# Weight pool first in SBUF, tiles begun at multiples of 2048 bytes, and a 2 KB scratch for dynamic DMAs

## The chip, the cores and the metric

The kernel runs on one core of one Trainium2 chip. The metric is the device time of one execution in microseconds (us); lower is better. Before the change the median of 3 runs was 2548.22 us (2548.09 to 2548.79).

## The reference

Two transformer blocks, one after the other, on 256 tokens of width 2048, all in float32. Cut to what matters here:

```python
# block 1
h = rms_norm(x, norm_mix_w);  proj = h @ w_in            # 2048 x 6160
y_a = chunked_band_attention(...);  y_g = rms_norm(gated_linear_attention(...)) * silu(r_g)
x = x + concat([y_a, y_g]) @ w_out                       # 2048 x 2048
u = causal_depthwise_conv(rms_norm(x) @ w_ffn_up)        # 2048 x 11264
x = x + (gelu(u_gate) * u_val) @ w_ffn_down              # 5632 x 2048
x = x + sigmoid(rms_norm(x) @ w_ple_gate) * (p @ w_ple_proj)
x = rms_norm(x, final_norm_w)
# block 2
z = rms_norm(x) @ w_in_2                                 # 2048 x 7168
x = x + concat([moba_attention(...), silu(rg) * retention(...)]) @ w_o_2
x = x + (silu(h2 @ w_gate_2) * (h2 @ w_up_2)) @ w_down_2
x = x + (p_2 @ w_ple_proj_2) * sigmoid(rms_norm(x) @ w_ple_gate_2 + b_ple_gate_2)
```

Nearly all the work is in the products with weight matrices, every one of which is read once.

## The kernel before

**Numbers in two parts.** Each float32 operand of a large product is split into a high part (rounded to the type fp32r, which TensorE multiplies in one pass) and a low part (the rest, also fp32r). A product is high times high, plus low times high, plus high times low.

**The weight stream.** The weights lie in HBM in the order of use, as 881 tiles of 128 partitions x 1024 numbers (4096 bytes in a partition). `load` (L148) brings one into a buffer `raw` (4 buffers), `split_hi` (L156, ScalarE) makes the high part `wh` (5 buffers), `split_lo` (L167, VectorE) the low part `wl` (4 buffers). Each call of `slot` does this for tiles some places ahead, so that TensorE finds its tile ready. The order of all instructions on all engines is written by the program itself, in one pass.

**The activations.** The other operand of each product lies in a *region*, a tile of 128 partitions x 8 x 2 x 256 numbers (16 KB in a partition): 8 k-tiles, each of 2048 bytes, the high part of 256 tokens and then the low part. There are five places for regions, R0 to R4, used again and again under other names:

| place | names that stand in it, in order of use (the profile leaves the numbers at a name's end out: f10, f11, f22, f23 are all f; g102 is g; hp0 is hp) |
|---|---|
| R0, R1 | h0a, h0b; f10, f11; hp0, hp1; R1: keys and queries; y2a, y2b; g200, g201 and g210, g211 |
| R2 | y1a; g102, g112; m2a; f22; hp2 |
| R3 | keys and queries; g103, g113; m2b; f23; hp3 |
| R4 | the gated linear attention's tiles; y1b; g104, g114; keys and queries; g204, g214 |

**The two forms of product.** All of them go through `mm` (L222), and each matmul loads its own stationary operand (LDWEIGHTS).

- *Narrow* products, `prod_b` (names `acc<-f,wh`, `acc<-f,wl` and so on): the weights are stationary, 128 x 128 (512 bytes in a partition), the activations move. For each k-tile and each of 2 blocks of output columns there is a pair: a matmul of 512 columns (stationary from `wh`, moving the whole k-tile) and one of 256 columns (stationary from `wl`, moving its high half).
- *Wide* products, `prod_a` (names `acc<-wh,m2a` and so on): the activations are stationary, 512 or fewer columns of a weight tile move. For each k-tile and half of the tokens there are three matmuls: `wh`, `wl`, `wh`.

`prod_p`, in the per-layer embedding, is narrow with 256 columns: for each stationary tile the moving operand is first the high half, then the low half of a k-tile of `ph`, then the high half again.

**Where a tile lies.** A pool hands out space in the order in which its tags are first asked for, each at a multiple of 32 bytes. The pools open in the order `sp` (all tiles but the weights'), `wp` (`raw`, `wh`, `wl`), above a scratch of 16,384 bytes for dynamic DMAs and 128 bytes of constants. Adding up the sizes gives each tile's first byte in its partition: R0 begins at 16,384 + 128 + 1,984 (vec) + 512 (ident) + 512 (ones) + 16,384 (X) = 35,904. A k-tile is 2048 bytes, a stationary slice 512, a weight tile 4096, so that all k-tiles of a region, and all slices of a tile, have the same remainder by 128.

Of the kernel before, what the change touches and what calls it, by code (L numbers as in the profile page):

```python
# [5 lines left out]
F32 = mybir.dt.float32  # L6
# [6 lines left out]
P = 128  # L13
# [6 lines left out]
NEG = -1e30  # L20
MIX_ORDER = (0, 1, 2, 3, 8, 9, 10, 11, 4, 5, 6, 7, 12, 13, 14, 15)
HALVES = ((0, 24), (24, 44))


def weight_plan():
    """The weight tiles in the order of use: (k-tiles, column ranges).

    Wide tiles have 2 k-tiles of 512 columns (moving operand), narrow ones
    4 k-tiles of 256 columns (stationary operand).
    """  # L30
    tiles = []
    full = tuple(range(KT))

    def gemm(n, kts, chunks):
        for ch in chunks:
            for i in range(0, len(kts), n):
                tiles.append((kts[i : i + n], ch))

    def even(name, lo, hi, step):
        return [[(name, c, c + step)] for c in range(lo, hi, step)]  # L40

    def wide(name, lo, hi):
        gemm(2, full, even(name, lo, hi, 512))

    def narrow(name, lo, hi, kts=full):
        gemm(4, kts, even(name, lo, hi, 256))

    def ffn(gate, up, off, down):
        for a, b in HALVES:
            gemm(4, full, [[(gate, c * P, c * P + P), (up, off + c * P, off + c * P + P)] for c in range(a, b)])  # L50
            narrow(down, 0, D, tuple(range(a, b)))

    def ple(gate, proj):
        for c in range(0, D, 512):
            narrow(gate, c, c + 512)
            gemm(2, (0, 1), even(proj, c, c + 512, 512))

    gemm(2, full, [[("w_in", 4096, 4608)], [("w_in", 4608, 4864)], [("w_in", 4864, 5120), ("w_in", 6144, 6160)]])
    narrow("w_in", 3072, 4096)
    narrow("w_in", 0, 2048)  # L60
    wide("w_in", 2048, 3072)
    wide("w_in", 5120, 6144)
    narrow("w_out", 0, D, MIX_ORDER)
    ffn("w_ffn_up", "w_ffn_up", FF, "w_ffn_down")
    ple("w_ple_gate", "w_ple_proj")
    wide("w_in_2", 0, 3072)
    narrow("w_in_2", 3072, 5120)
    wide("w_in_2", 5120, 7168)
    narrow("w_o_2", 0, D)
    ffn("w_gate_2", "w_up_2", 0, "w_down_2")  # L70
    ple("w_ple_gate_2", "w_ple_proj_2")
    return tiles


def plan_offsets(tiles):
    out, off = [], 0
    for kts, ch in tiles:
        f = len(kts) * sum(b - a for _, a, b in ch)
        out.append((off, f))
        off += P * f  # L80
    return out, off
# [16 lines left out]
class Net:  # L98
# [4 lines left out]
    def __init__(self, nc, tc, pools, ins, out):  # L103
        self.nc, self.tc = nc, tc
        self.sp, self.wp, self.ps = pools
        self.ins, self.out = ins, out
        self.plan = weight_plan()
        self.offs, _ = plan_offsets(self.plan)
        self.i = 0
        self.raw, self.H, self.L = {}, {}, {}  # L110
        self.ev, self.side = [], []
        self.done = set()
        self.nacc = 0
        self.forced = []

# [1 line left out]
    def t(self, tag, shape, dt=F32, bufs=1, name=None):  # L117
        return self.sp.tile(shape, dt, tag=tag, name=name or tag, bufs=bufs)

    def psum(self, tag, bufs):  # L120
        return self.ps.tile([P, 512], F32, tag=tag, name=tag, bufs=bufs)
# [10 lines left out]
    def pv(self):  # L132
        return self.psum("pv", 1)

# [1 line left out]
    def cut(self, i, part):  # L136
        f = self.offs[i][1]
        return slice(0, f) if part is None else slice(part * f // 2, (part + 1) * f // 2)
# [37 lines left out]
        assert len(self.plan[i][0]) == nk  # L176
        return self.H.pop(i), self.L.pop(i), self.offs[i][1] // nk

# [1 line left out]
    def step(self, q, g):  # L180
        try:
            next(g)
        except StopIteration:
            q.remove(g)
# [25 lines left out]
        while key not in self.done:  # L210
            yield

# [1 line left out]
    def begin_chunk(self):  # L214
        c = self.nacc
        self.nacc += 1
        if c >= 2:
            self.need(("acc", c - 2))
        return c, self.acc()
# [45 lines left out]
                    self.mm(o, x[:, ls], H[:, sl], False, g + j == nk - 1)  # L265

    def join(self, acc, dst):
        """dst = the sum of both halves of a narrow chunk's accumulators."""
        m = self.v2(self.t("tq", [P, 512], bufs=2))
        self.nc.scalar.activation(m, acc[:, :, T:], AF.Copy)  # L270
        yield
        self.nc.vector.tensor_add(dst, m, acc[:, :, :T])
# [4 lines left out]

        self.ev.append(self.freeing(c, evict(acc)))

# [1 line left out]
    def v2(self, ap):  # L281
        return ap.rearrange("p (b t) -> p b t", b=2)

# [43 lines left out]
    def acts_of(self, regions, n, key):  # L327
        return [(regions[k // 8][:, k % 8].rearrange("p a t -> p (a t)"), (key, k)) for k in range(n)]
# [34 lines left out]

        return rc, rb, run()

# [1 line left out]
    def consts(self):  # L367
        nc, ins = self.nc, self.ins
        self.vec = self.t("vec", [P, NV])
        self.ident = self.t("ident", [P, P])  # L370
        self.ones = self.t("ones", [P, P])
        nc.gpsimd.memset(self.ones, 1.0)
        nc.scalar.activation(self.ident[:, 0:1], self.ones[:, 0:1], AF.Copy)
        nc.scalar.dma_start(self.vec[:, 0:16], ins["vec"][:, 0:16])
        self.X = self.t("X", [P, KT, T])
# [69 lines left out]
        while self.ev or self.side:  # L445
            self.tick()

# [1 line left out]
    def mix1(self, acts):  # L449
        nc = self.nc  # L450
        rc, rb = self.rc, self.rb
# [335 lines left out]
        self.done.add(("go", 3))  # L787
        yield

# [1 line left out]
    def ffn(self, blk):  # L791
        nc = self.nc
        hk = self.hkey
        acts = self.acts_of(self.hR, KT, hk)
        regs = (2, 3, 4) if blk == 1 else (0, 1, 4)
        hn = (0, 1) if blk == 1 else (2, 3)
        rb, rskey = self.rb, (hk, "rs")
        key = f"p{blk}"
        for half, (a, b) in enumerate(HALVES):
            G = [self.region(r, f"g{blk}{half}{r}") for r in regs]  # L800
            gk = f"g{blk}{half}"
            for c in range(a, b):
                ev = self.ev_glu1 if blk == 1 else self.ev_glu2
                self.chunk("B", acts, ev(c, c - a, G, gk, rb, rskey))
            gacts = self.acts_of(G, b - a, gk)
            if half:
                self.side.append(self.embed(blk))
                if blk == 1:
                    self.side.append(self.rope_tables())
                R = [self.region(r, f"hp{r}") for r in hn]  # L810
                sq = self.new_sq()
                self.rc, self.rb, rs = self.row_scale(sq, (key, "rs"))
            for c in range(8):
                n, acc = self.begin_chunk()
                self.prod_b(gacts, acc)
                if half:
                    self.ev.append(self.ev_resid(n, acc, c, R, sq, "norm_ple_w" if blk == 1 else "g_ple_2", key, rs))
                else:
                    self.ev.append(self.ev_add(n, acc, c))
        self.hR, self.hkey = R, key  # L820
# [52 lines left out]
            yield from self.put_g(G, gk, cl, w[:, 1, :])  # L873
        return ev

# [1 line left out]
    def embed(self, blk):  # L877
        nc = self.nc
        s8 = self.t("S8a", [P, 2, 1024], name="pr")
        ph = self.t("S8b", [P, 4, 2, T], F32R, name="ph")  # L880
        pr = self.v2(s8[:, 0, 0:512])
        nc.sync.dma_start(pr, self.ins[f"pT{blk}"])
        self.emb = s8, ph
        for _ in range(12):
            yield
        nc.scalar.activation(ph[:, 0:2, 0, :], pr, AF.Copy)
        yield
        nc.vector.tensor_sub(ph[:, 0:2, 1, :], pr, ph[:, 0:2, 0, :].bitcast(F32))
        self.done.add(("emb", blk))
# [82 lines left out]
            yield  # L972
        self.done.add(("ple", blk, c))

# [1 line left out]
    def rope_tables(self):  # L976
        nc, ins = self.nc, self.ins
        tabs = self.tabs = self.t("g4", [P, 4, 2, P], name="tabs")
# [332 lines left out]
def pack(inputs):  # L1311
    g = {k: np.asarray(v) for k, v in inputs.items()}
    mats = {k: g[k][0] for k in (
        "w_in", "w_out", "w_ffn_up", "w_ffn_down", "w_ple_gate", "w_ple_proj", "w_in_2", "w_o_2",
        "w_gate_2", "w_up_2", "w_down_2", "w_ple_gate_2", "w_ple_proj_2")}
    plan = weight_plan()
    offs, total = plan_offsets(plan)
    flat = np.empty(total, np.float32)
# [28 lines left out]


def body(nc, tc, ins, out):
    with tc.tile_pool(name="sp", bufs=1) as sp, tc.tile_pool(name="wp", bufs=1) as wp, \  # L1350
            tc.tile_pool(name="ps", bufs=1, space=PSUM) as ps:
        with tc.manual_schedule():
            net = Net(nc, tc, (sp, wp, ps), ins, out)
            net.build()
    return net
# [16 lines left out]
```

## Time and profile before

| | before |
|---|---|
| median of 3 runs | 2548.22 us (2548.09 to 2548.79) |
| span of the profiled execution, first to last instruction | 2547.2 us |
| the profiled execution's time as the runs count it | not given on the page; the runs' median is 1.0 us above its span |
| TensorE (PE) busy | 2534.5 us, 100% of the span |
| weight loads of TensorE (PEld) busy | 2184.4 us, 86% |
| VectorE (DVE) busy | 1668.3 us, 65% |
| ScalarE (ACT) busy | 1282.9 us, 50% |
| GpSimd (POOL) busy | 8.3 us |
| weight DMAs, share of the 16 engines' time | 54.1% |
| granted TensorE clock, mean | 0.999 |

TensorE's matmuls are pipelined, so that the lengths of neighbours overlap and "busy" says only that no gap was left. What a matmul costs is read from the distance between starts: so many matmuls between two starts, so much time.

### The profile page before, as it was taken

How to read it: one execution, taken by the hardware profiler on the slowest of the kernel's cores; microseconds unless marked ns; L12 is line 12 of the kernel's file. 1: busy time of each engine (PE TensorE's matmuls, PEld its weight loads, DVE VectorE, ACT ScalarE, POOL GpSimd, SP SyncE). 2: the span in 40 equal slices, each digit the busy share in tenths (PEclk: the TensorE clock that was granted, in tenths of full speed). 3: DMA queues.
4: the chain of work that ended last, by engine and by line, in shares of the span. 5: the costliest groups of instructions: out<-in, count | busy, mean ns of one | idle time of the engine just before them, and what ended most of it. 6: DMA issues, size and time to landing. Idle time of an engine off the chain costs nothing.

```text
span 2547.2 us, 36496 instructions
## 1 busy us (share of the span) xinstructions
PE 2534.5 (100%) x14162; PEld 2184.4 (86%) x14162; DVE 1668.3 (65%) x2374; ACT 1282.9 (50%) x1713; POOL 8.3 (0%) x60
## 2 busy tenths in 40 slices
PE   8999999999999999999999999999999999999999
PEld 7887788888888888888878888888888888888888
DVE  6655567777755777767886775666666555666665
ACT  6534544655543565545544544444444334444443
POOL 0000000000000000000000000000000000000000
PEclk9999999999999999999999999999999999999999
DMA  7545355555555555555555455555555555555554
GB/s 242 183 142 178 131 177 188 187 186 190 190 189 188 186 190 190 192 193 187 189 174 188 161 177 189 174 187 189 188 188 189 190 190 189 187 188 193 190 193 147
DMA packets 133550, 469.30 MB, mean 184 GB/s; under 512 B 14960, under 2 KB 17392, under 8 KB 133376
## 3 DMA queue, kind: packets, MB, share of 16 engines
q1 hardware_dynamic: 133232, 466.95, 54.1%
q8 instruction: 111, 1.82, 0.3%
q14 instruction: 63, 0.52, 0.1%
q10 hardware_dynamic: 144, 0.01, 0.0%
HBM read 464.80 MB, written 2.10 MB: 183 GB/s over the span
## 4 chain that ended last, share of the span: by engine, by line
PE 99%; DMA 0%; DVE 0%; ACT 0%; issue 0%; SPq 0%; ACTq 0%
PE acc L222 95%; PE sc L222 2%; PE pv L222 1%; PE tr L650 0%; DMA raw<-weights 0%; PE sc L1099 0%; ACT wh L156 0%; PE sc L1182 0%; PE sc L528 0%; DVE ty L948 0%; SPq L390 0%; DVE wl L167 0%; DVE X L949 0%; PE tr L737 0%; SPq L148 0%
## 5 line engine op out<-in xcount | busy, mean ns | idle before, releaser
L167 DVE TENSOR_TENSOR wl<-raw,wh 128x1024 fp32r<-128x1024 f32 (+1 forms) x881 | 1068.8, 1214 | 830.6 <-PE acc L222 538.6
L156 ACT ACTIVATE wh<-raw 128x1024 fp32r<-128x1024 f32 (+1 forms) x881 | 924.7, 1050 | 905.7 <-PE acc L222 729.8
L222 PE MATMUL acc<-f,wh 128*128 128x512 f32 x2816 | 984.3, 393 | 0.0
L222 PE MATMUL acc<-f,wl 128*128 128x256 f32 x2816 | 786.2, 279 | 0.0
L222 PEld LDWEIGHTS acc<-f,wh 128*128 128x128 f32 x2816 | 528.0, 187 | 123.9
L222 PEld LDWEIGHTS acc<-f,wl 128*128 128x128 f32 x2816 | 528.3, 188 | 0.0
L222 PE MATMUL acc<-g,wh 128*128 128x512 f32 x1408 | 491.0, 393 | 0.0
L222 PE MATMUL acc<-g,wl 128*128 128x256 f32 x1408 | 393.2, 279 | 0.0
L222 PEld LDWEIGHTS acc<-g,wh 128*128 128x128 f32 x1408 | 264.1, 188 | 61.1
L222 PEld LDWEIGHTS acc<-g,wl 128*128 128x128 f32 x1408 | 264.3, 188 | 0.0
L222 PE MATMUL acc<-hp,wh 128*128 128x512 f32 x512 | 179.9, 394 | 0.0
L222 PE MATMUL acc<-hp,wl 128*128 128x256 f32 x512 | 143.0, 279 | 0.0
L222 PEld LDWEIGHTS acc<-hp,wh 128*128 128x128 f32 x512 | 96.0, 188 | 22.2
L222 PE MATMUL acc<-wh,m2b 128*128 128x512 f32 x320 | 104.5, 398 | 0.0
L222 PE MATMUL acc<-wh,m2a 128*128 128x512 f32 x320 | 104.4, 399 | 0.0
L222 PEld LDWEIGHTS acc<-hp,wl 128*128 128x128 f32 x512 | 96.1, 188 | 0.0
L849 ACT ACTIVATE ty<-tU,vec 128x256 f32<-128x256 f32 x88 | 48.1, 595 | 75.1 <-DVE tU L845 75.1
L270 ACT ACTIVATE tq<-acc 128x512 f32<-128x512 f32 x124 | 71.9, 580 | 4.9 <-PE acc L222 4.9
L222 PE MATMUL acc<-wh,h0a 128*128 128x512 f32 (+2 forms) x224 | 68.1, 380 | 5.7 <-ACT wh L156 5.7
L222 PEld LDWEIGHTS acc<-wh,m2a 128*128 128x128 f32 x320 | 60.3, 188 | 14.2
L222 PEld LDWEIGHTS acc<-wh,m2b 128*128 128x128 f32 x320 | 60.1, 188 | 14.1
L222 PE MATMUL acc<-h0a,wh 128*128 128x512 f32 x192 | 68.6, 397 | 0.0
(272 smaller groups left out, 2780.6 us busy)
## 6 DMA issues: line engine op xcount, KB each, us to landing
raw<-weights SPq DMA_DIRECT2D x863, 512.0 KB, 3.4
raw<-weights SPq DMA_DIRECT2D x10, 256.0 KB, 2.8
raw<-weights SPq DMA_DIRECT2D x8, 272.0 KB, 2.8
aB<-bias SPq DMA_DIRECT2D x8, 256.0 KB, 3.5
X<-xT SPq DMA_DIRECT2D x7, 256.0 KB, 6.6
dk<-decay SPq DMA_DIRECT2D x8, 192.0 KB, 3.7
out<-X SPq DMA_DIRECT2D x6, 256.0 KB, 2.8
pr<-pT SPq DMA_DIRECT2D x2, 256.0 KB, 4.2
```

The lines of the kernel that those rows point to most:

```text
L156: self.nc.scalar.activation(self.H[i][:, a], self.raw[i][:, a], AF.Copy)
L167: self.nc.vector.tensor_sub(self.L[i][:, a], r[:, a], self.H[i][:, a].bitcast(F32))
L222: self.nc.tensor.matmul(out, lhsT, rhs, start=start, stop=stop, skip_group_check=True, **kw)
L270: self.nc.scalar.activation(m, acc[:, :, T:], AF.Copy)
L849: nc.scalar.activation(y[:, b, :], u[:, b, 0:T], AF.Identity, scale=self.col("cw0", j), bias=self.col("b_ffn_conv", j))
```

## The change

The pool of the weights is opened first. Scratch for dynamic DMAs shrinks from 16,384 to 2,048 bytes. `t` keeps count of the space handed out, and puts a filling tile ahead of each new tile of 8192 bytes or more, so that it begins at a multiple of 2048; the same is done once ahead of the weight pool. No instruction is added, removed or moved: the streams of all engines read the same but for line numbers and the numbers at the ends of names. What differs is the addresses. (The diff also drops a docstring and some comments; those pieces are left out below.)

```diff
+ALIGN = 2048
+SCRATCH = 2048
...
         self.forced = []
-
-    # ---- tiles ----
+        self.sizes = {}
+        self.off = SCRATCH + 128
+        self.pad(self.wp)
+        self.off += 13 * 4096
+
+
     def t(self, tag, shape, dt=F32, bufs=1, name=None):
+        size = -(-4 * int(np.prod(shape[1:])) // 32) * 32
+        if tag not in self.sizes:
+            if size >= 8192:
+                self.pad(self.sp)
+            self.sizes[tag] = size
+            self.off += size * bufs
         return self.sp.tile(shape, dt, tag=tag, name=name or tag, bufs=bufs)
+
+    def pad(self, pool):
+        n = -self.off % ALIGN
+        if n:
+            name = f"pad{self.off}"
+            pool.tile([P, n // 4], F32, tag=name, name=name, bufs=1)
+            self.off += n
...
 def body(nc, tc, ins, out):
-    with tc.tile_pool(name="sp", bufs=1) as sp, tc.tile_pool(name="wp", bufs=1) as wp, \
+    with tc.tile_pool(name="wp", bufs=1) as wp, tc.tile_pool(name="sp", bufs=1) as sp, \
             tc.tile_pool(name="ps", bufs=1, space=PSUM) as ps:
...
-    nc = _bacc.Bacc("TRN2", target_bir_lowering=False, num_devices=1)
+    nc = _bacc.Bacc("TRN2", target_bir_lowering=False, num_devices=1, dynamic_dma_scratch_size=SCRATCH)
```

The first byte of the tiles that the products read, added up as above, and its remainder by 128 and by 2048:

| tile | before: first byte, by 128, by 2048 | after: first byte, by 128, by 2048 |
|---|---|---|
| `raw`, 4 buffers of 4096 | 174,816; 96; 736 | 4,096; 0; 0 |
| `wh`, 5 buffers of 4096 | 191,200; 96; 736 | 20,480; 0; 0 |
| `wl`, 4 buffers of 4096 | 211,680; 96; 736 | 40,960; 0; 0 |
| R0 | 35,904; 64; 1088 | 77,824; 0; 0 |
| R1 | 52,288; 64; 1088 | 94,208; 0; 0 |
| R2 | 144,704; 64; 1344 | 190,464; 0; 0 |
| R3 | 73,344; 0; 1664 | 116,736; 0; 0 |
| R4 | 97,920; 0; 1664 | 141,312; 0; 0 |
| S8b, where `ph` stands | 89,728; 0; 1664 | 133,120; 0; 0 |

## Rows read from the trace of the kernel before

**Rows 1.** The page, busy time and share of the span by engine.

```profile
span 2547.2 us, 36496 instructions
PE 2534.5 (100%) x14162; PEld 2184.4 (86%) x14162; DVE 1668.3 (65%) x2374; ACT 1282.9 (50%) x1713; POOL 8.3 (0%) x60
```

**Rows 2.** The page, the chain that ended last, shares by engine.

```profile
PE 99%; DMA 0%; DVE 0%; ACT 0%; issue 0%; SPq 0%; ACTq 0%
```

**Rows 3.** Waits of PE: waiting, waited for, us in total, times, longest.

```profile
PE acc L222 <- ACT wh L156: 5.7, 2, 4.5
```

**Rows 4.** PE's groups: out<-in, columns, count | busy us, mean ns | idle.

```profile
L222 PE MATMUL acc<-f,wh 128*128 128x512 f32 x2816 | 984.3, 393 | 0.0
L222 PE MATMUL acc<-g,wh 128*128 128x512 f32 x1408 | 491.0, 393 | 0.0
L222 PE MATMUL acc<-hp,wh 128*128 128x512 f32 x512 | 179.9, 394 | 0.0
...
L222 PE MATMUL acc<-h0a,wh 128*128 128x512 f32 x192 | 68.6, 397 | 0.0
...
L222 PE MATMUL acc<-wl,m2a 128*128 128x512 f32 x160 | 63.4, 396 | 0.0
...
L222 PE MATMUL acc<-wh,h0a 128*128 128x512 f32 x160 | 56.0, 418 | 5.7 <-ACT wh L156 5.7
...
L222 PE MATMUL acc<-y1a,wh 128*128 128x512 f32 x128 | 45.7, 395 | 0.0
```

**Rows 5.** Timeline of PE, block 2's first products: start us, length us, instruction.

```profile
1494.34 0.39 PE L222 MATMUL acc<-m2b,wh 128*128 128x512 f32 x1
...
1499.88 0.40 PE L222 MATMUL acc<-m2a,wh 128*128 128x512 f32 x1
...
1505.49 0.39 PE L222 MATMUL acc<-m2b,wh 128*128 128x512 f32 x1
...
1511.04 0.40 PE L222 MATMUL acc<-wh,m2a 128*128 128x512 f32 x1
...
1522.28 0.40 PE L222 MATMUL acc<-wh,m2b 128*128 128x512 f32 x1
...
1533.46 0.39 PE L222 MATMUL acc<-wh,m2a 128*128 128x512 f32 x1
...
1544.71 0.40 PE L222 MATMUL acc<-wh,m2b 128*128 128x512 f32 x1
```

**Rows 6.** Chain of work in order of time: start us, length us, what.

```profile
444.42 732.23 PE acc L222 x4192
...
1720.65 731.03 PE acc L222 x4192
```

**Rows 7.** Timeline of PE, one product with `ph`.

```profile
1264.47 0.40 PE L222 MATMUL sc<-ph,wh 128*128 128x256 f32 x2
1264.70 0.28 PE L222 MATMUL sc<-ph,wl 128*128 128x256 f32 x1
...
1267.34 0.40 PE L222 MATMUL acc<-wh,m2a 128*128 128x512 f32 x1
```

**Rows 8.** Timeline of PE near the start.

```profile
13.34 0.63 PE L222 MATMUL acc<-wl,h0a 128*128 128x512 f32 x1
13.77 1.06 PE L222 MATMUL acc<-wh,h0a 128*128 128x512 f32 x2
14.62 0.61 PE L222 MATMUL acc<-wl,h0a 128*128 128x512 f32 x1
```

**Rows 9.** Busy us by stretch: PE, PEld, DVE, ACT, POOL, then granted clock, DMA share, GB/s.

```profile
12.50:14.90 2.40, 2.40 (x7) 1.94 (x6) 2.08 (x4) 1.90 (x4) 0.00 (x0) 0.50 1.03 414
...
1494.30:1505.50 11.20, 11.20 (x67) 9.82 (x66) 8.54 (x11) 4.74 (x5) 0.00 (x0) 1.00 0.56 188
```

**Rows 10.** Who waited for whom, all engines: us in total, times, longest.

```profile
ACT wh L156 <- PE acc L222: 729.8, 500, 3.9
DVE wl L167 <- PE acc L222: 538.6, 471, 2.9
```

## The prediction

> **What bounds the kernel now.** First the page's busy times, then its chain, then TensorE's waits. PE is busy for 2534.5 of 2547.2 us [rows 1], it makes up 99% of the chain that ended last [rows 2], and its longest waits are two on the split of the first weights, 5.7 us in all, near the start [rows 3]. ScalarE and VectorE run ahead: both wait longest for PE to free their buffers, 729.8 and 538.6 us in total [rows 10]. So the time is the sum of the distances between matmul starts, and a nanosecond (ns) off a matmul counts fully, up to a limit that a gain of some per cent doesn't reach.
>
> The counts come from the groups by form [rows 4]: narrow pairs (512 columns with `wh`, 256 with `wl`) are 2,816 for f, 1,408 for g, 512 for hp, 192 each for h0a and h0b (not shown, the same form), and 128 for each of y1a, y1b, m2a, m2b, y2a, y2b (one is shown): 5,888 pairs, 11,776 matmuls. Wide matmuls of 512 columns: 160 with `wl` for each of m2a, m2b and twice that with `wh`, 80 with `wl` and 160 with `wh` for each of h0a and h0b: 1,440. Some 192 wide ones of 256 or 272 columns are left.
>
> [...] But in the stretch that begins at 1494.34 us, at clock 1.00 [rows 9], 16 pairs take 5.54 us with m2b, then 5.61 with m2a, then 5.55 with m2b [rows 5]: 346.3, 350.6 and 346.9 ns a pair. [...]
>
> **Where the addresses show.** m2a stands in R2, whose remainder by 128 is 64, m2b in R3, remainder 0. All else is alike: 16 pairs, the same weight buffers, the same stretch. So a moving operand with remainder 0 is cheaper by 350.6 - 346.6 = 4.0 ns a pair. A second place to read it is the long piece of chain in each feed-forward, 4,192 matmuls or 2,096 pairs: 732.23 us in block 1, 731.03 in block 2 [rows 6]. By the table of places, block 1 has R3 and R4 (remainder 0) in 256 + 192 = 448 of its pairs, block 2 in 704 (f23) + 192 = 896. So 448 pairs are worth 1.20 us, 2.7 ns each. I take 3.3, between the two, with 2.7 and 4.0 as bounds.
>
> The wide products tell of the stationary operand: there the regions are stationary and the weights move (remainder 96 by 128). 48 matmuls take 11.24 us with m2a, 11.18 with m2b, 11.25 with m2a [rows 5]: 234.3 against 232.9 ns. Here remainder 0 is worth 1.4 ns a matmul; I use 1.2: the starts are given to 0.01 us, which is 0.2 ns a matmul.
>
> **The change part by part.**
>
> *No instruction changes*, so there is nothing to add for filling tiles, pools or scratch. [...]
>
> *Moving regions in R0, R1, R2 go from remainder 64 to 0.* By the table of places these hold 1,408 + 704 of f, 768 of g, 384 of hp, 384 of h0, and y1a, m2a, y2a, y2b: 4,160 pairs. The other 1,728 are at 0 already. 4,160 x 3.3 = 13.7 us, between 11.2 and 16.6.
>
> *Moving weights of the wide products go from remainder 96 to 0.* No row shows a 512-column matmul with both at 0. The nearest is the m2b pair less its 256-column half. [...] The wide ones then go from 234.3 (h0a, h0b, m2a: 960) and 232.9 (m2b: 480) to 229: 960 x 5.3 + 480 x 3.9 = 7.0 us, and half a us for the 192 narrower ones. 7.5 us, between 0 (if a moving weight tile gains nothing) and 10.
>
> *Stationary weights of the narrow products go from remainder 96 to 0.* The trace shows 64 to 0 in wide products only, 1.2 ns for 512 columns. I take 1.2 for the 512-column half and 0.6 for the other: 5,888 x 1.8 = 10.6 us, and 1.2 x 1,440 = 1.7 us for the wide ones, whose 229 above still had a stationary operand at 96. 12.3 us; between 0 (the load is hidden under the matmul before) and 25 (twice as much, if 96 is worse than 64).
>
> *The weights' DMAs and splits* also get aligned buffers. Both are ahead of PE [rows 10], so I put it at nothing; at the start, the 5.7 us wait [rows 3] could move by a fraction of a us.
>
> Sum: 13.7 + 7.5 + 12.3 = 33.5 us off a span of 2547.2, and 1.0 us from span to the runs' median: 2548.2 - 33.5, about **2515 us**. With the bounds of the terms the likeliest case runs from 2497 to 2537.
>
> [...]
>
> **The rivals.**
>
> *Nothing changes (2548 us).* The m2a and m2b difference could belong to the place and not to the remainder: R3 and R4 both lie between 73,344 and 114,304, and after the change R0 and R1 take that stretch. Against it: R1 reaches up to 68,672, R2 begins at 144,704, and both sides of the stretch cost the same in the feed-forwards. Should place decide, the 1,728 pairs with R3 and R4 lose 3.3 ns and the 2,816 with R0 and R1 (1,408 of f, 512 of g, 256 of hp, 384 of h0, 256 of y2) gain it: 3.6 us, within 0.2%, which is about what runs of this kernel can tell from no change.
>
> [...]
>
> [...]
>
> *Slower: both operands on the same remainder collide.* After the change the stationary slice and the moving k-tile both begin at a multiple of 512, so their reads, which run at the same time, could meet in the same part of SBUF at each step. Now their difference by 128 is 96 or 32. If meeting costs as much as alignment gives and as much again, 6.6 ns a pair instead of the gain of term three, the pairs lose 5,888 x 6.6 - 13,700 = 25 us net, and after the wide ones' 7.5 the time is about 2566 us. It decides from 3.6 ns a pair up. Against it: narrow products are cheaper at a difference of 32 than of 96, wide ones at 96 than at 32 [rows 5], so the difference does not rule now.
>
> **How the numbers follow.** Partial gain as summed: 0.59. Much more goes: 0.19. Nothing changes: 0.13. Slower: 0.09. The predicted time is that of the first, 2515. The range reaches down into half of the second case, 2440, and up over the third, 2549; some 0.1 lies below and 0.1 above. Faster by over 0.2% (under 2543): 0.78, within 0.2%: 0.13, slower: 0.09.
>
> **What would show it.** In the changed kernel's timeline, m2a and m2b should cost the same, about 345 ns a pair and 228 a wide matmul; the two feed-forward pieces should be equal and near 722 us (345 x 2,096). If m2a falls to 346.6 and m2b stays, the stationary term was nothing (some 2527 us). If wide matmuls stay at 233, it is the stationary operand alone that counts there. If both stand at 350, the place or the collision decides. I would be wrong above all if alignment by more than 128 matters, which no row shows, or if PE, freed, began to wait for splits.

## The result and the profile after

The changed kernel is slower: 2562.78 us, median of 4 runs (2562.35 to 2564.11), against 2548.15 of before beside it, ratio 1.0057 with an interval of 1.0043 to 1.0072. The forecast was 2515.

| | after | against before |
|---|---|---|
| span of the profiled execution | 2562.3 us | +15.1 |
| PE busy | 2550.0 us | +15.5 |
| VectorE, ScalarE busy | 1668.0, 1282.9 us | -0.3, 0 |
| granted clock | 0.999 | the same |

The page of after, busy times by engine, as in [rows 1]:

```profile
span 2562.3 us, 36496 instructions
PE 2550.0 (100%) x14162; PEld 2190.6 (85%) x14162; DVE 1668.0 (65%) x2374; ACT 1282.9 (50%) x1713; POOL 8.4 (0%) x60
```

PE is still the whole path, and takes longer for the same matmuls. Where, the chain in order of time tells, as in [rows 6] (start us, length us, what):

```profile
444.67 740.59 PE acc L241 x4192
...
1725.32 740.59 PE acc L241 x4192
```

The two feed-forwards, 732.23 and 731.03 us before, now are equal, as they should be with regions alike, but at 740.59: 353.3 ns a pair instead of 349.3 and 348.8. Then the timeline of PE at the place of [rows 5]:

```profile
1500.04 0.40 PE L241 MATMUL acc<-m2b,wh 128*128 128x512 f32 x1
...
1505.70 0.40 PE L241 MATMUL acc<-m2a,wh 128*128 128x512 f32 x1
...
1511.35 0.40 PE L241 MATMUL acc<-m2b,wh 128*128 128x512 f32 x1
...
1517.00 0.40 PE L241 MATMUL acc<-wh,m2a 128*128 128x512 f32 x1
...
1527.94 0.39 PE L241 MATMUL acc<-wh,m2b 128*128 128x512 f32 x1
...
1538.82 0.39 PE L241 MATMUL acc<-wh,m2a 128*128 128x512 f32 x1
```

m2a and m2b cost the same now, 353.1 ns a pair each (5.65 us / 16; the first 16 took 5.66), where they cost 350.6 and 346.6. The wide matmuls went the other way: 48 of m2b take 10.88 us, 226.7 ns each, where m2a took 234.3 and m2b 232.9. The first 48, with m2a, take 10.94. So narrow pairs lose 4,160 x 3.4 + 1,728 x 6.1 = 24.7 us (from 349.9 and 347.2, which is what [rows 6] give for the two kinds of region, to 353.3), wide matmuls give back at most 960 x 7.6 + 480 x 6.2 = 10.3, and the difference, 14.4 us, is what the runs show (14.6).

One more thing is seen in single steps. The timeline of PE in block 1's second up product (the 512-column half of each pair; the matmuls with `wl` lie between):

```profile
900.30 0.40 PE L241 MATMUL acc<-f,wh 128*128 128x512 f32 x1
...
900.65 0.40 PE L241 MATMUL acc<-f,wh 128*128 128x512 f32 x1
...
901.01 0.40 PE L241 MATMUL acc<-f,wh 128*128 128x512 f32 x1
...
901.36 0.40 PE L241 MATMUL acc<-f,wh 128*128 128x512 f32 x1
```

Three pairs take 1.06 us, 353.3 ns each, 0.35, 0.36 and 0.35. The timeline shows no wait of PE among them, and the engines beside PE come and go at times of their own (ScalarE's split starts at 899.73 us, VectorE's at 900.01). Here PE's stream runs in a fixed rhythm, and the question is what sets it.

### The profile page after: what moved, and what is told of

It is laid out like the page before. It is cut to its first block, busy times and chain, and to the rows that moved or that the text cites. A ratio compares the mean times of both kernels' runs of the same rounds, so it can differ in the third digit from the quotient of the medians.

```text
span 2562.3 us, 36496 instructions
## 1 busy us (share of the span) xinstructions
PE 2550.0 (100%) x14162; PEld 2190.6 (85%) x14162; DVE 1668.0 (65%) x2374; ACT 1282.9 (50%) x1713; POOL 8.4 (0%) x60
## 4 chain that ended last, share of the span: by engine, by line
PE 99%; DMA 0%; DVE 0%; ACT 0%; issue 0%; SPq 0%; ACTq 0%
PE acc L241 95%; PE sc L241 2%; PE pv L241 1%; PE tr L669 0%; DMA raw<-weights 0%; PE sc L1118 0%; ACT wh L175 0%; PE sc L1201 0%; PE sc L547 0%; DVE ty L967 0%; SPq L409 0%; DVE wl L186 0%; DVE X L968 0%; PE tr L756 0%; SPq L167 0%
## 5 line engine op out<-in xcount | busy, mean ns | idle before, releaser
L241 PE MATMUL acc<-f,wh 128*128 128x512 f32 x2816 | 995.7, 399 | 0.0
L241 PE MATMUL acc<-g,wh 128*128 128x512 f32 x1408 | 497.7, 399 | 0.0
L241 PEld LDWEIGHTS acc<-wh,m2a 128*128 128x128 f32 x320 | 60.1, 188 | 12.3
```

What stands on the lines that cost most here:

```text
L241: self.nc.tensor.matmul(out, lhsT, rhs, start=start, stop=stop, skip_group_check=True, **kw)
```

## The experiments

In what follows *weights* stands for the remainder by 128 of the first byte of `wh` and `wl`, *regions* for that of R0 to R4 and S8b, and *difference* for weights less regions, by 128. Before, the difference was 32 where regions are at 64, 96 where they are at 0; after, it is 0.

**1. Undo the weights' alignment alone.** The pad takes a remainder; e1, e2, e3, e4 and e12 differ in its numbers only.

```diff
-        self.pad(self.wp)
+        self.pad(self.wp, WREM)
...
-                self.pad(self.sp)
+                self.pad(self.sp, RREM.get(tag, 0))
...
-    def pad(self, pool):
-        n = -self.off % ALIGN
+    def pad(self, pool, rem):
+        n = (rem - self.off) % ALIGN
...
+WREM = 96
+RREM = {}
```

> The changed kernel with the weight pool moved up by 96 bytes, so that weights begin at remainder 96 by 128 as before and the regions stay at 0. Meeting theory (narrow pairs are dear when stationary slice and moving k-tile begin at the same remainder): all pairs as m2b before, 346.6 to 347.2 ns, wide matmuls as m2b before, 233: 5,888 x 346.8 + 1,440 x 233 + the 155 us of the rest of before = 2533 us, faster than before. Weight theory (stationary weights at remainder 0 are dear, wherever the regions are): the same 2533. Place theory (the pools' new order is what costs): pairs stay at 353 ns and the wide ones at 228 or 233, about 2563 to 2570 us.

Measured: 2532.18 us (before 2548.24), ratio 0.9938 (0.9923 to 0.9953), faster. The chain's feed-forward piece, and the wide products in PE's timeline:

```profile
440.66 726.62 PE acc L243 x4192
```

```profile
1499.85 0.39 PE L243 MATMUL acc<-wh,m2a 128*128 128x512 f32 x1
...
1511.04 0.40 PE L243 MATMUL acc<-wh,m2b 128*128 128x512 f32 x1
```

726.62 / 2,096 = 346.7 ns, in all regions, and 11.19 us / 48 = 233.1 ns a wide matmul. So the first term of the prediction (regions from 64 to 0) holds while the weights stay at 96: 16.1 us were measured, some 1 us of it in the wide matmuls with R0 to R2 (234.3 to 233.1 ns, 960 of them), and 13.7 were forecast. The pools' order is not what costs.

**2. Undo the regions' alignment instead.**

```diff
+WREM = 0
+RREM = {'R0': 64, 'R1': 64, 'R2': 64, 'R3': 64, 'R4': 64, 'S8b': 64}
```

> The changed kernel with the weights at remainder 0 and the regions (R0 to R4 and S8b) begun 64 bytes later, at remainder 64. Meeting theory: the two no longer begin at the same remainder, pairs at or under the 350 ns of before, 2535 to 2550 us. Weight theory: pairs stay at 353 ns, about 2563 us. Place theory: 353 ns, 2563 us. In all of them the wide matmuls, with moving weights at 0, are near 228 to 229 ns.

Measured: 2570.13 us, ratio 1.0086 (1.0071 to 1.0101), the slowest of all. The chain, and the wide products:

```profile
444.42 740.58 PE acc L243 x4192
```

```profile
1531.59 0.39 PE L243 MATMUL acc<-wh,m2b 128*128 128x512 f32 x1
...
1542.79 0.39 PE L243 MATMUL acc<-wh,m2a 128*128 128x512 f32 x1
```

Pairs at 353.3 ns with no common remainder (in the four products with m2a and m2b ahead of the wide ones some 349: 64 pairs take 22.17 us, from 1498.21 in the chain to 1520.38 in PE's timeline, and 22.45 in the changed kernel, at 353.1 ns a pair): the meeting theory, in the form that only equal remainders cost, falls. And wide matmuls at 11.20 us / 48 = 233.3 ns, though their moving operand begins at 0: an aligned moving operand is not enough, against what all theories had expected.

**3. The change's places with the old remainders.**

```diff
+WREM = 736
+RREM = {'X': 1088, 'R0': 1088, 'R1': 1088, 'R2': 1344, 'R3': 1664, 'R4': 1664, 'S8b': 1664, 'S8a': 256}
```

> The changed kernel's pool order and its 2 KB scratch, but every tile padded to the remainder by 2048 that it had before (weights 736, R0 and R1 1088, R2 1344, R3, R4 and S8b 1664). Meeting and weight theory: only the remainders count, so the time is that of before, 2548 us within 0.1%, with m2a at 350 and m2b at 347 ns a pair. Place theory: it is as slow as the changed kernel, 2563 us, or the m2a and m2b times are exchanged.

Measured: 2548.06 us beside 2548.24, ratio 1.0000 (0.9990 to 1.0009). Its chain repeats [rows 6] to two hundredths of a us:

```profile
443.92 732.22 PE acc L243 x4192
...
1720.05 731.01 PE acc L243 x4192
```

Pools' order, places and the smaller scratch cost nothing. Only the remainders count; this settles the place theory and the rival "nothing changes".

**4. Both at 64.**

```diff
+WREM = 64
+RREM = {'R0': 64, 'R1': 64, 'R2': 64, 'R3': 64, 'R4': 64, 'S8b': 64}
```

> The changed kernel with weights and regions all begun 64 bytes later: both at remainder 64, difference 0. Meeting theory: as slow as the changed kernel, pairs 353 ns or, as moving operands at 64 were dearer before, 355; 2563 to 2575 us. Weight theory: stationary weights are off 0 again, pairs near 350 ns, about 2545 us. Place theory: 2563 us.

Measured: 2561.05 us, ratio 1.0049 (1.0034 to 1.0064). The chain's piece is 740.58 us as after, and the wide products in PE's timeline are at 10.88 us / 48 = 226.7 ns, as after:

```profile
1524.67 0.39 PE L243 MATMUL acc<-wh,m2b 128*128 128x512 f32 x1
...
1535.55 0.39 PE L243 MATMUL acc<-wh,m2a 128*128 128x512 f32 x1
```

So nothing depends on remainder 0 as such: (64, 64) does what (0, 0) does in the feed-forwards, and the weight theory falls too. What the five placements go by in their long stages is the difference. Wide matmuls: 226.7 ns at difference 0, 233 to 234 at 32, 64 and 96. Narrow pairs: 346.7 at 96, 350 at 32, 353.3 at 0 and 64. (One stretch of this run, at the start of block 1's feed-forward, is faster; it is shown under 9 to 11.)

**5 to 7. Maps of the difference.** Three kernels with regions at 0 in which each stage of the feed-forwards has its weights' start set apart, by longer buffers and an offset in them.

```diff
+WIDE, NARROW = (0, 0), (96, 96)
+STAGES = ((0, 0), (32, 32), (64, 64), (96, 96), (128, 128), (160, 160), (192, 192), (224, 224))
...
+def starts(kts, ch):
+    if len(kts) == 2 and "proj" not in ch[0][0]:
+        return WIDE
+    name, col, _ = ch[0]
+    if name in ("w_ffn_up", "w_gate_2", "w_ffn_down", "w_down_2"):
+        down = "down" in name
+        half = kts[0] >= 24 if down else col >= 24 * P
+        return STAGES[4 * name.endswith("_2") + 2 * half + down]
+    return NARROW
...
-            self.H[i] = self.wp.tile([P, 1024], F32R, tag="wh", name="wh", bufs=5)
+            o = starts(*self.plan[i])[0] // 4
+            self.H[i] = self.wp.tile([P, 1088], F32R, tag="wh", name="wh", bufs=5)[:, o : o + 1024]
...
-            self.L[i] = self.wp.tile([P, 1024], F32R, tag="wl", name="wl", bufs=4)
+            o = starts(*self.plan[i])[1] // 4
+            self.L[i] = self.wp.tile([P, 1088], F32R, tag="wl", name="wl", bufs=4)[:, o : o + 1024]
```

> Regions at remainder 0; buffers of wh and wl 256 bytes longer, so that a tile can begin anywhere in them. Wide products' weights begin at 0; the feed-forwards' weights begin at 0, 32, 64, 96 (block 1: up and down of the first half, up and down of the second) and 128, 160, 192, 224 (block 2, in the same order); all other narrow weights at 96. Difference theory (a narrow pair's time follows from the start of its weights less that of its region, by 128): pairs of 353, 350, 353, 347 ns in block 1 and the same four in block 2; wide matmuls 228; 2546 us in all. Odd-32 theory (only whether the two starts differ by an odd or an even multiple of 32 counts, and the region at 64 was dear by itself): 353, 347, 353, 347, twice; 2543 us. If it goes by 256 and not by 128, block 2's stages differ from block 1's.

> As the map before, but high and low weight tiles begin apart. (wh, wl) in the stages in the same order: (96, 0), (96, 32), (96, 64), (0, 96), (32, 96), (64, 96), (96, 96), (0, 32). If both loads count alike: 350, 348, 350, 350, 348, 350, 347, 352 ns a pair. If only the load that runs beside the 512-column matmul counts (that of the wl slice that comes after it): 353, 350, 353, 347, 347, 347, 347, 350. If only the wh slice's counts: 347, 347, 347, 353, 350, 353, 347, 353.

> As the first map, with starts between the multiples of 32, the same for wh and wl: 80, 112, 88, 104 in block 1, 16, 48, 92, 100 in block 2. If a read is of 64 or 32 bytes and only which of them begins a slice counts, 80 and 88 go as 64 (353) or as 96 (347), 112, 104 and 100 as 96 (347), 16 as 0 (353), 48 as 32 (350), 92 as 64. If the time follows the difference smoothly, 88 to 104 lie near 347, 80 and 112 near 350. If there is a start better than 96, one of them is under 346.

One run each: 2537.43, 2533.58 and 2537.05 us. The stages are read from PE's timeline, from the first matmul of one to the first of the next; they have 768, 384, 640 and 320 pairs. For the first of a block 0.9 us are taken off, for eight small matmuls of the row scale in it (four products in plain float32, each of which shows as two matmuls in the timeline, where one in fp32r shows as one). The equal map:

```profile
421.06 0.40 PE L256 MATMUL acc<-f,wh 128*128 128x512 f32 x1
...
688.42 0.39 PE L256 MATMUL acc<-g,wh 128*128 128x512 f32 x1
...
824.09 0.39 PE L256 MATMUL acc<-f,wh 128*128 128x512 f32 x1
...
1050.21 0.40 PE L256 MATMUL acc<-g,wh 128*128 128x512 f32 x1
...
1161.14 0.39 PE L256 MATMUL acc<-hp,wh 128*128 128x512 f32 x1
...
1690.19 0.40 PE L256 MATMUL acc<-f,wh 128*128 128x512 f32 x1
...
1960.73 0.42 PE L256 MATMUL acc<-g,wh 128*128 128x512 f32 x1
...
2095.18 0.39 PE L256 MATMUL acc<-f,wh 128*128 128x512 f32 x1
...
2318.46 0.40 PE L256 MATMUL acc<-g,wh 128*128 128x512 f32 x1
...
2429.41 0.39 PE L256 MATMUL acc<-hp,wh 128*128 128x512 f32 x1
```

The fine one, its first stages (80, 112, 88):

```profile
421.04 0.40 PE L256 MATMUL acc<-f,wh 128*128 128x512 f32 x1
...
693.25 0.39 PE L256 MATMUL acc<-g,wh 128*128 128x512 f32 x1
...
828.92 0.39 PE L256 MATMUL acc<-f,wh 128*128 128x512 f32 x1
...
1052.91 0.39 PE L256 MATMUL acc<-g,wh 128*128 128x512 f32 x1
```

| map | ns a pair, by start of the weights, in the order of the stages |
|---|---|
| equal | 0: 347.0; 32: 353.3; 64: 353.3; 96: 346.7; 128: 351.1; 160: 350.1; 192: 348.9; 224: 346.7 |
| `wh`, `wl` apart | (96, 0): 346.8; (96, 32): 352.0; (96, 64): 353.3; (0, 96): 346.7; (32, 96): 346.7; (64, 96): 353.3; (96, 96): 346.7; (0, 32): 346.7 |
| fine | 80: 353.3; 112: 353.3; 88: 350.0; 104: 349.5; 16: 346.7; 48: 346.7; 92: 348.9; 100: 348.9 |

Neither the difference theory nor the odd-32 theory gives the equal map. The starts 96 and 224 are at 346.7 both, but the first stage, with weights and regions at 0 as in the changed kernel, runs at 347.0 and not at 353.3, and 128, 160 and 192 don't repeat 0, 32 and 64. So 128 is not shown to be the period. The expectation's third branch, by 256, fits in part: by 256 the kernel before had differences of 160 (R0 to R2) and 96 (R3, R4), and the map's 160 is at 350.1 as those regions were at 350.0, its 32 at 353.3. But 192 is at 348.9 here and was at 353.3 in e2 (0 less 64), so that 256 doesn't settle it either. Of the map with `wh` and `wl` apart none of the three lists holds: as a test of which load counts it is inconclusive. The fine map shows that it doesn't go by whole 32 bytes: around 96 the time rises on both sides, 346.7, 348.9 (4 bytes off), 350.0 and 349.5 (8), 353.3 (16), while 16 and 48, far off, are at 346.7 again. No stage is under 346.7.

**8. The version that the runs pointed to.** As the equal map, without stages: regions at 0, wide weights at 0, narrow weights at 96.

```diff
+WIDE, NARROW = (0, 0), (96, 96)
...
+def starts(kts, ch):
+    if len(kts) == 2 and "proj" not in ch[0][0]:
+        return WIDE
+    return NARROW
```

> The version that the runs so far point to: regions at 0, weights of wide products at 0, of narrow products at 96. Difference theory: all narrow pairs 346.7 and all wide matmuls 228 ns, so 5,888 x 346.7 + 1,440 x 228 + 155 = 2525 us, under both kernels. Theory that the wide products gained by the weights' place alone: wide 233, 2532 us.

Measured: 2525.24 us beside 2548.14, ratio 0.9910 (0.9894 to 0.9927). Its chain and its wide products:

```profile
440.49 726.62 PE acc L250 x4192
```

```profile
1507.13 0.39 PE L250 MATMUL acc<-wh,m2b 128*128 128x512 f32 x1
...
1518.01 0.39 PE L250 MATMUL acc<-wh,m2a 128*128 128x512 f32 x1
```

726.62 / 2,096 = 346.7 ns a pair and 10.88 us / 48 = 226.7 ns a wide matmul: both forms at the best seen, and 0.9% under the kernel before.

**9 to 11. Why the same addresses ran at 347.0 and at 353.3.** Two reasons offered themselves: the map's buffers are 4352 bytes apart and not 4096, or the stream keeps a rhythm that it came in with. e9 is e8 with

```diff
-WIDE, NARROW = (0, 0), (96, 96)
+WIDE, NARROW = (0, 0), (0, 0)
```

> All weights and regions at remainder 0 by 128, as in the changed kernel, but the buffers of wh and wl 4352 bytes apart, as in the maps. The first map's stage at (0, 0) ran at 347 ns a pair, the changed kernel at 353. Memory theory (at difference 0 the stream has a fast and a slow rhythm, and keeps the one that it came in with; the map's stage came from weights at 96, which are always fast): here nothing is at 96, so slow, 353 ns, about 2562 us. Distance theory (4352 bytes between buffers, so that neighbours differ by 256, is what made the map's stage fast): 347 ns, about 2525 us.

Measured: 2562.21 us, ratio 1.0058 (1.0037 to 1.0078); block 1's feed-forward piece in the chain is 740.59 us, 353.3 ns a pair. The distance of the buffers is not it. e10 and e11 have the map's edit with buffers of 1152 numbers and

```diff
+WIDE, NARROW = (0, 0), (96, 96)
+STAGES = ((0, 0), (0, 0), (0, 0), (0, 0), (96, 96), (0, 0), (96, 96), (0, 0))
```

and e11 differs from e10 in one line:

```diff
-WIDE, NARROW = (0, 0), (96, 96)
+WIDE, NARROW = (0, 0), (64, 64)
```

> Buffers of wh and wl 4608 bytes apart (a multiple of 512). Wide weights at 0. Block 1's feed-forward: narrow weights at 0 in all four stages; block 2's: 96, 0, 96, 0; all other narrow weights at 96. Memory theory: the stages at 0 come from stages at 96 and keep their 347 ns, 2525 us in all, or fall to 353 where something breaks the rhythm. Distance theory: the 2,816 pairs at 0 take 353 ns, 2543 us.

> The same but for one thing: the narrow weights outside the feed-forwards begin at 64, not 96, so that block 1's feed-forward has the same addresses as in the run beside it and comes from a slow stage. Memory theory: 353 ns in block 1's feed-forward, 347 in block 2's stages at 0 that follow a stage at 96, about 2550 us. Distance theory: block 1's feed-forward as in the run beside it.

Measured: 2529.14 us (ratio 0.9928, 0.9908 to 0.9948) and 2553.97 us (1.0024, 1.0013 to 1.0036). PE's timeline of the first, stages of block 1 and then of block 2:

```profile
688.58 0.39 PE L256 MATMUL acc<-g,wh 128*128 128x512 f32 x1
...
821.70 0.39 PE L256 MATMUL acc<-f,wh 128*128 128x512 f32 x1
...
1950.66 0.40 PE L256 MATMUL acc<-g,wh 128*128 128x512 f32 x1
...
2086.34 0.39 PE L256 MATMUL acc<-f,wh 128*128 128x512 f32 x1
```

and of the second, block 1:

```profile
699.12 0.40 PE L256 MATMUL acc<-g,wh 128*128 128x512 f32 x1
...
834.79 0.40 PE L256 MATMUL acc<-f,wh 128*128 128x512 f32 x1
```

Block 1's first down product, 384 pairs, has the same addresses in both. It takes 133.12 us, 346.7 ns a pair, in e10, whose narrow weights outside the feed-forwards are at 96, and 135.67 us, 353.3 ns, in e11, where they are at 64. The long piece of the chain does the same, 726.63 us in e10 (shown below) against 740.58 in e11:

```profile
444.88 740.58 PE acc L256 x4192
```

So at difference 0 there are (at least) two rhythms, one of them ran for more than 700 us, and which one it was hung on what ran before.

But the stream did not keep the rhythm that it came in with, as the memory theory has it. In e10 block 1's feed-forward follows weights at 96, and its first 32 pairs ran slow all the same: 11.31 us, 353.4 ns each, up to the first four of the row scale's small matmuls.

```profile
421.21 0.40 PE L256 MATMUL acc<-f,wh 128*128 128x512 f32 x1
...
432.52 0.61 PE L256 MATMUL pv<-ones,sq 128*128 128x128 f32 x4
```

Behind these small matmuls the chain has 16 pairs in 5.56 us, and behind the next four the long piece at 346.7 ns a pair:

```profile
433.13 5.56 PE acc L256 x32
...
439.13 726.63 PE acc L256 x4192
```

The first stage of the equal map did the same (its first 32 pairs take 11.31 us, 421.06 to 432.37), which makes its 347.0. In e4, with both starts at 64, it went the other way. The last 240 pairs with y1a and y1b and the first 32 of block 1's feed-forward ran at 94.30 us / 272 = 346.7 ns, and behind the same small matmuls the stream was slow, 5.66 us for 16 pairs and then 740.58:

```profile
340.63 94.30 PE acc L243 x544
...
435.37 5.66 PE acc L243 x32
...
441.47 740.58 PE acc L243 x4192
```

So in these three kernels the rhythm changed where small matmuls broke the stream; in e11 it came in slow and stayed slow through the same break. Block 2 fits this: there the stages at 0 that follow a stage at 96 are slow from their start, as in block 1, and no small matmuls stand in them (135.68 and 135.69 us for 384 pairs in e10 and e11). That is the 4 us by which each run is over what the memory theory gave: (384 + 320) x 6.6 ns = 4.6. What decides at such a break stays open.

**12. Difference 96 the other way round.**

```diff
+WREM = 0
+RREM = {'R0': 32, 'R1': 32, 'R2': 32, 'R3': 32, 'R4': 32, 'S8b': 32}
```

> The changed kernel with all regions begun 32 bytes later: weights at 0, regions at 32, so that weights less region is 96 by 128, as where weights are at 96 and regions at 0. Difference theory: all narrow pairs 346.7 ns, wide matmuls 233 (their two starts differ), 2532 us. Theory that weights at an odd multiple of 32 are needed: 353 ns, about 2570 us.

Measured: 2532.34 us, ratio 0.9942 (0.9925 to 0.9958), the time of e1. The chain:

```profile
440.54 726.64 PE acc L243 x4192
```

Weights at 0 are as good as any when the regions are 32 bytes on, and the wide matmuls lose their 226.7 ns again, as their two starts differ: the chain's 48 at 1293.60 us take 11.19 us, 233.1 ns each, and the same 48 took 10.94 in the changed kernel. In all seven kernels that had whole stages of the feed-forwards at the difference 96, those ran at 346.7 ns, whatever ran before.

## Why the prediction was wrong

- *What bounds the kernel* was right: PE's distances between starts are the time, before and after, and neither the splits nor the DMAs took part (in the changed kernel's chain PE has 99%, ScalarE, VectorE and the DMAs 0%). Also right was that no cost hangs on the pools' order or the scratch (e3, 1.0000).
- *"So a moving operand with remainder 0 is cheaper"* is where it broke. The rows were read rightly, 350.6 against 346.6 ns, and the size is nearly right as long as the weights stay at 96 (e1: 16.1 us, some 1 of it in wide matmuls, for the 13.7 forecast), but the reason was put in one operand's own alignment, when it is how the two operands' starts stand to each other. R3 was cheap because the weights stood 96 bytes past it, by 128.
- *The stationary term* ("from remainder 96 to 0", 12.3 us gained) therefore had the wrong sign: it moves the difference from 96 to 0, and costs 5,888 x 6.6 = 39 us from e1's state, less 1,440 x 6.4 = 9 us that the wide matmuls gain. The runs show 30.6 us (2562.78 - 2532.18, not beside the same runs of before), which is the first term's 16.1 and the 14.6 by which the changed kernel is slower. (In the fast rhythm that the difference 0 can have, the term would be nothing: 346.7 ns at both.)
- *The wide term* (7.5 us) had the right size: no run shows the 229 ns that it is added up with, but 226.7 at difference 0 (after, e4, e8) and 233 to 234 at the others. That is up to 10.3 us by the m2a and m2b rows, 7 by e8 against e1 (2532.18 - 2525.24; they did not run beside the same runs of before). Its reason was wrong as well: e2 has its moving operand at 0 and stays at 233.3, e4 has it at 64 and is at 226.7. Equal starts are what counts there.
- *The rival "slower"* came nearest to what the runs show, a cost that goes by one operand's start against the other's (353.3 ns a pair at difference 0, 346.7 at 96), and, at 2566 us, to the time. That the two reads collide was its guess. That its 6.6 ns a pair is the size measured is luck: it was taken as twice the 3.3 of the alignment, with no row behind it. It was given 0.09 by one step: "narrow products are cheaper at a difference of 32 than of 96, wide ones at 96 than at 32 [rows 5], so the difference does not rule now". There the difference is the moving start less the stationary one, so that its sign turns from one form to the other. Counted as weights less regions, as here, the same rows have both forms cheaper at 96 (m2b) than at 32 (m2a), and speak for the difference. Nor need both forms have the same best one: wide products are best at 0, narrow ones at 96. But the rival was wrong in part too: 64 is as dear as 0 (353.3 ns in e2), and 0 itself can run fast (346.7 in e10).
- *"Much more goes"* (0.19), with the 2440 at the lower end of the range, falls too: no run shows a saving of that size, and the fastest kernel took 2525.24 us (e8). With both operands at 0 a pair takes 353.3 ns in the changed kernel, not less. And in e1 no moving k-tile crosses a multiple of 2048, in e12 every one does, while both run at 346.7 ns a pair.

What is shown: how the two starts stand to each other changes the time, and not the alignment of either. Moving the weights alone by 96 bytes (e1) or the regions alone by 32 (e12) takes the changed kernel's narrow pairs from 353.3 to 346.7 ns; moving both by 64 (e4) leaves the feed-forwards' long pieces as they were. Wide matmuls were at 226.7 ns at difference 0 in the changed kernel, e4 and e8, narrow pairs at 346.7 at difference 96 in seven kernels. At 0 narrow pairs ran in two rhythms, 346.7 and 353.3 ns (e10, e11), and the changed kernel's feed-forwards run in the slow one; in the fast one it would be near 2524 us (an estimate: 2562.8 less 5,888 x 6.6 ns), about the time of e8. No rule is shown for the other differences: by 128, 32 ran at 350.0 (before) and 353.3 (the equal map), 64 at 353.3 and, as 192, at 348.9.

The weight loads run beside the matmuls (in the changed kernel one starts at 900.31 us beside a matmul that starts at 900.30), but that the two reads meet in SBUF was not shown. No run took the weight loads away, so what makes the difference between 346.7 and 353.3 ns stays open, and so does why `wh` and `wl` apart (96, 64) are slow and (0, 96) fast.

## What to carry to other kernels

Where TensorE streams without a gap and matmuls of one form take longer with one tile than with another (here 350.6 and 346.6 ns a pair), the starts of stationary and moving tiles are worth an experiment of their own: choose the difference of the two starts for each form of product, and not "aligned" for its own sake (2525.24 us in e8, 2562.78 with all at 0), and keep to one at which the fast rhythm holds whatever came before (here 96, at 346.7 ns in seven kernels). A row that shows that one of two placements is cheaper does not tell which property of it is the reason; placements with both operands shifted by the same amount (e4 here) tell alignment from difference, and cost one run. And the same addresses can run in another rhythm after another stage (346.7 ns in e10, 353.3 in e11), or after a few small matmuls in between (353.4 ns ahead of them in e10, 346.7 behind), so a map of many settings in one kernel has to be checked against kernels with a single one.

## What the runs showed that was not expected

Many stages of narrow pairs sit on steps: 346.7, 350.0 and 353.3 ns came back in stages of hundreds of pairs, 3.3 ns apart. Between them lie 348.9 (three stages), 349.5, 351.1 and 352.0 (one each). Identical addresses ran at 346.7 and at 353.3 for nearly the whole length of a feed-forward, and eight small matmuls near its start could turn the one into the other. Shifting the weights by 4 bytes from the best start (96 to 92 or 100) costs 2.2 ns a pair, by 16 bytes 6.6, while starts of 16 and 48 are as fast as 96; each of these starts was one stage in one run, and whether it holds after other stages was not tested.
